# A hybrid decoder layer in split float32: feed-forward and per-layer gate by Strassen's scheme of seven products

## The chip, the core and the metric

The kernel runs on one core of one Trainium2 chip. The metric is the device time of one execution in microseconds (us), as a median of several runs. The core has TensorE for matmuls (PE in the profile; PEld is the loading of its stationary operand), VectorE (DVE), ScalarE (ACT), GpSimd (POOL) and SyncE (SP), whose queue issues nearly all transfers here. Matmul results stand in PSUM, in 8 banks of 128 x 512 float32.

## The reference

One decoder layer over 512 tokens of width 2048, all in float32:

```python
h = rms_norm(x, g_mix); z = h @ w_in
...                                     # attention and retention, 8 heads each
x = x + concatenate([a_out, r_out], axis=-1) @ w_o
h2 = rms_norm(x, g_ffn)
x = x + (silu(h2 @ w_gate) * (h2 @ w_up)) @ w_down        # 2048 -> 5632 -> 2048
gate = sigmoid(rms_norm(x, g_ple) @ w_ple_gate + b_ple_gate)   # 2048 -> 2048
x = x + (p @ w_ple_proj) * gate                           # 256 -> 2048
```

## The kernel before

Matmuls of full precision are made of three of the fast float32r kind. `split` (L50) writes a tile as H + L: ScalarE copies it to float32r (H, L54), VectorE subtracts (L, L55). `mm3` (L74) adds aH·bH, aH·bL and aL·bH in PSUM (L75 to L77), each 128 x 128 stationary against up to 512 moving columns. Weights arrive as units of 512 KB (128 x 1024 float32): `weights` (L60) loads one into `raw` from the SP queue and splits it into `wh` and `wl`, which have three buffers.

The residual stream lies in `xt` as 16 tiles [128 dims, 512 tokens], and `gained` (L127) makes the split activations `actH`, `actL` of a norm's input from it. `cols` (L101) computes [columns, tokens]: weights stationary, activations moving, four banks `acc` of 128 columns, which the last unit finishes one after the other. The norm's factor per token (`bc`) is multiplied in when a bank is read.

The feed-forward (L442 on) goes over 11 slices of 512 hidden columns. A slice is a `cols` for the gate (8 units), one for the up projection (8 units), and, one slice later, the down projection: four `cols` of 2 units each, whose banks are added into `xt` (L123). That is 192 matmuls each, 576 in a slice. Then come four column slabs of the per-layer gate (L490 on): `w_pp` with the embeddings `pTH` (24 matmuls), `w_pg` with the normed x (192), and the sigmoid with its products and the store. `tc` is a Tile context: it puts in the semaphores and orders each engine's instructions by its own estimate of the times. Every engine, and the SP queue, works through its list in order.

Of the kernel before, what the change touches and what calls it, by code (L numbers as in the profile page):

```python
# [33 lines left out]
def layer_kernel(ctx, tc, xT, pT, g_mix, wqk, wv, wg, qk_norm, g_ret, w_o, g_ffn,  # L34
                 w_gate, w_up, w_down, g_ple, w_pg, b_pg, w_pp,
                 ident_c, rope_c, ropeT_c, decay_c, mask_c, outT):
# [5 lines left out]
    actp = ctx.enter_context(tc.tile_pool(name="actp", bufs=NC))  # L42
    xp = ctx.enter_context(tc.tile_pool(name="xp", bufs=1))
    wp = ctx.enter_context(tc.tile_pool(name="wp", bufs=3))
    raw_pools = [ctx.enter_context(tc.tile_pool(name="rawp", bufs=2))]
    acc_p = ctx.enter_context(tc.tile_pool(name="acc_p", bufs=4, space=PSUM))
    tp_p = ctx.enter_context(tc.tile_pool(name="tp_p", bufs=2, space=PSUM))
    at_p = ctx.enter_context(tc.tile_pool(name="at_p", bufs=2, space=PSUM))

# [1 line left out]
    def split(H, L, src, scale=None):  # L51
        """H + L = src * scale, H the leading 12 bits of it and L the rest, exactly."""
# [21 lines left out]
    def mm3(o, aH, aL, bH, bL, start, stop):  # L74
        nc.tensor.matmul(o, aH, bH, start=start, stop=False)  # L75
        nc.tensor.matmul(o, aH, bL, start=False, stop=False)  # L76
        nc.tensor.matmul(o, aL, bH, start=False, stop=stop)  # L77
# [4 lines left out]
    def rows(units, act, evac, kc=2, then=None):  # L82
        """[tokens, columns]: the sum over the units' chunks, a bank for each token block."""
# [17 lines left out]
    def cols(units, act, evac, kc=2, late=1):  # L101
        """[columns, tokens]: a bank for each 128 columns, which the last units finish one by one."""
# [42 lines left out]
    def rms_of(src, parts, tmp, n, r):  # L145
        """Over the partitions of src: r[t, b] = (mean of token b * 128 + t + eps) ** -0.5."""
# [10 lines left out]
    def over_partitions(r):  # L157
        """[P, NB] -> every token's value on every partition."""
# [17 lines left out]
    bias = consts.tile([P, NC], F32)  # L176
# [6 lines left out]
    mix_ctx = ExitStack()  # L183
    mixp = mix_ctx.enter_context(tc.tile_pool(name="mixp", bufs=3))
    ap = mix_ctx.enter_context(tc.tile_pool(name="ap", bufs=1))

    # keeps the tensor engine busy from the start on, so that its clock gate opens
# [24 lines left out]
    bc1 = stat.tile([P, T], F32, name="bc", tag="bc", bufs=1)  # L212
# [3 lines left out]
    def load_rest():  # L216
# [4 lines left out]
        nc.sync.dma_start(bias, b_pg)  # L221
# [50 lines left out]
    def qk_attn(i, then=None):  # L272
        """q and k of a pair of heads as [tokens, d]: projection, norm, rotation."""
# [69 lines left out]
    def qk_ret(i):  # L343
        """q and k of a pair of heads as [d, tokens]: projection, norm, rotation."""
# [86 lines left out]
    h2T = []  # L431
    total = rp_tile("total")

    def after2(k):
        h2T.append(gained(k, gf))
# [3 lines left out]
    bc = stat.tile([P, T], F32, name="bc", tag="bc", bufs=1)  # L439
    norm_of(total, two_rm(), stat.tile([P, NB], F32, name="rs"), bc)  # L440
    mix_ctx.close()

# [1 line left out]
    h3T = []  # L444
    ep = ctx.enter_context(tc.tile_pool(name="ep", bufs=1))
    rawp2 = ctx.enter_context(tc.tile_pool(name="rawp2", bufs=2))
    total = ep.tile([P, T], F32)
    pTH = [[ep.tile([P, T], F32R, name=f"p{k}{part}") for part in "HL"] for k in range(2)]
    with tc.tile_pool(name="fp", bufs=1) as fp:
        for k in range(2):  # L450
            raw = fp.tile([P, T], F32, name="praw", tag="t", bufs=3)
            nc.sync.dma_start(raw, pT[k * P:(k + 1) * P, :])
            split(*pTH[k], raw)

        def after3(k):
            h3T.append(gained(k, gp))
            squares(total, k, ep.tile([P, T], F32, name="sq", bufs=2))

        def down(s, aT):
            add_into_x(lambda n: [w_down[2 * s + u, n] for u in range(2)], aT,  # L460
                       after3 if s == FS - 1 else None)

        prev = None
        for s in range(FS):
            sil, aT = [], []
            if s == 1:
                raw_pools.append(rawp2)
# [119 lines left out]
```

## Time and profile before

| | |
|---|---|
| median of 3 runs | 2536.45 us (2535.67 to 2536.95) |
| span of the profiled execution | 2533.9 us |
| TensorE busy | 2523.8 us, 12028 matmuls |
| VectorE busy | 1175.5 us |
| ScalarE busy | 733.8 us |
| HBM read / written | 241.47 MB / 4.19 MB |

The span runs from the first to the last instruction of the profiled execution; its time as a run counts some 2.5 us more around it. A matmul's duration in the trace overlaps with the next one's, so that the distance between starts, not the duration, tells how long TensorE needs for it.

### The profile page before, as it was taken

The page shows a single profiled execution, that of the slowest core. Times are in us where ns is not written, and L with a number is a line of the kernel's source. Part 1 is how long each engine was busy: PE and PEld are TensorE (multiplying, and loading weights), DVE is VectorE, ACT ScalarE, POOL GpSimd, SP SyncE. Part 2 cuts the span into 40 slices and gives each one's busy share as a digit, 9 for nine tenths or more (in the row PEclk, how much of TensorE's full clock was granted, in tenths as well). Part 3 has the DMA queues.
Part 4 walks back from the last instruction along what each step waited for, and adds up shares of the span by engine and source line. Part 5 has one row for each costly group of instructions (what it writes and reads, how often), then busy time and mean ns, then how long its engine had stood idle before and what let it go on. Part 6 is the DMA issues. An engine that isn't in the chain of part 4 may idle for free.

```text
span 2533.9 us, 29210 instructions
## 1 busy us (share of the span) xinstructions
PE 2523.8 (100%) x12028; PEld 2123.6 (84%) x12028; DVE 1175.5 (46%) x1611; ACT 733.8 (29%) x1058; POOL 134.6 (5%) x107
## 2 busy tenths in 40 slices
PE   9999999999999999999999999999999999999999
PEld 7888888888888888888888888888888888888887
DVE  6575674636364763333334242424242424347334
ACT  5333332323232442212222222222222222225322
POOL 1122020000000010000000000000000000000000
PEclk9999999999999999999999999999999999999999
DMA  5222222333323232232332332332322223323332
GB/s 188 84 84 82 85 92 97 103 100 102 108 94 109 88 124 96 97 100 92 100 100 92 100 99 92 100 97 94 100 95 97 96 97 98 100 93 99 111 113 75
DMA packets 74404, 251.75 MB, mean 99 GB/s; under 512 B 9120, under 2 KB 9760, under 8 KB 74272
## 3 DMA queue, kind: packets, MB, share of 16 engines
q1 hardware_dynamic: 71568, 245.69, 29.6%
q10 hardware_dynamic: 2704, 4.20, 0.7%
q8 instruction: 94, 1.54, 0.2%
q14 instruction: 38, 0.31, 0.0%
HBM read 241.47 MB, written 4.19 MB: 97 GB/s over the span
## 4 chain that ended last, share of the span: by engine, by line
PE 98%; DVE 1%; DMA 1%; issue 0%; SPq 0%; ACT 0%; DVEq 0%
PE acc L76 31%; PE acc L75 31%; PE acc L77 31%; PE at L76 1%; PE at L77 1%; PE at L75 1%; DMA x<-in_xT 0%; PE tp L334 0%; PE tp L309 0%; DVE x L123 0%; DVE wl L55 0%; PE tp L150 0%; PE tp L161 0%; DVE actL L58 0%; DMA gf<-in_g_ffn 0%
## 5 line engine op out<-in xcount | busy, mean ns | idle before, releaser
L55 DVE TENSOR_TENSOR wl<-raw,wh 128x1024 fp32r<-128x1024 f32 (+1 forms) x445 | 551.7, 1240 | 1064.0 <-ACT wh L54 1062.9
L54 ACT ACTIVATE wh<-raw 128x1024 fp32r<-128x1024 f32 (+1 forms) x445 | 470.6, 1058 | 1418.9 <-PE acc L76 1157.9
L75 PE MATMUL acc<-actH,wh 128*128 128x512 f32 x2048 | 797.3, 389 | 0.0
L76 PE MATMUL acc<-actL,wh 128*128 128x512 f32 x2048 | 797.2, 389 | 0.0
L77 PE MATMUL acc<-actH,wl 128*128 128x512 f32 x2048 | 793.9, 389 | 0.0
L77 PEld LDWEIGHTS acc<-actH,wl 128*128 128x128 f32 x2048 | 384.4, 188 | 79.6
L76 PEld LDWEIGHTS acc<-actL,wh 128*128 128x128 f32 x2048 | 384.5, 188 | 79.3
L75 PEld LDWEIGHTS acc<-actH,wh 128*128 128x128 f32 x2048 | 384.4, 188 | 79.2
L75 PE MATMUL acc<-aH,wh 128*128 128x512 f32 x704 | 273.9, 389 | 0.0
L76 PE MATMUL acc<-aL,wh 128*128 128x512 f32 x704 | 273.9, 389 | 0.0
L77 PE MATMUL acc<-aH,wl 128*128 128x512 f32 x704 | 272.2, 389 | 0.0
L76 PE MATMUL acc<-wl,actH 128*128 128x256 f32 (+1 forms) x768 | 244.7, 320 | 1.1 <-DVE wl L55 1.1
L77 PE MATMUL acc<-wh,actL 128*128 128x256 f32 (+1 forms) x768 | 244.2, 320 | 0.0
L123 DVE TENSOR_TENSOR x<-acc,x 128x512 f32<-128x512 f32 x304 | 207.7, 688 | 77.9 <-PE acc L77 76.1
L75 PE MATMUL acc<-wh,actH 128*128 128x256 f32 (+1 forms) x768 | 240.5, 321 | 1.6 <-ACT wh L54 1.6
L76 PEld LDWEIGHTS acc<-wl,actH 128*128 128x128 f32 x768 | 146.6, 191 | 11.9 <-DVE wl L55 1.6
L75 PEld LDWEIGHTS acc<-wh,actH 128*128 128x128 f32 x768 | 145.3, 191 | 12.5 <-ACT wh L54 2.5
L76 PEld LDWEIGHTS acc<-aL,wh 128*128 128x128 f32 x704 | 132.2, 188 | 27.5
L75 PEld LDWEIGHTS acc<-aH,wh 128*128 128x128 f32 x704 | 132.1, 188 | 27.4
L77 PEld LDWEIGHTS acc<-aH,wl 128*128 128x128 f32 x704 | 132.1, 188 | 27.4
L77 PEld LDWEIGHTS acc<-wh,actL 128*128 128x128 f32 x768 | 146.1, 191 | 10.2
L474 POOL TENSOR_TENSOR sil<-sil,bc 128x512 f32<-128x512 f32 x44 | 66.3, 1540 | 1213.2 <-ACT sil L473 1213.2
(136 smaller groups left out, 1615.6 us busy)
## 6 DMA issues: line engine op xcount, KB each, us to landing
raw<-in_w_gate SPq DMA_DIRECT2D x88, 512.0 KB, 3.6
raw<-in_w_up SPq DMA_DIRECT2D x88, 512.0 KB, 3.6
raw<-in_w_down SPq DMA_DIRECT2D x88, 512.0 KB, 3.6
raw<-in_wqk SPq DMA_DIRECT2D x63, 512.0 KB, 3.6
raw<-in_wv SPq DMA_DIRECT2D x32, 512.0 KB, 3.7
raw<-in_w_o SPq DMA_DIRECT2D x32, 512.0 KB, 3.6
raw<-in_w_pg SPq DMA_DIRECT2D x32, 512.0 KB, 3.7
raw<-in_wg SPq DMA_DIRECT2D x16, 512.0 KB, 3.7
```

Source lines behind the costliest of these rows:

```text
L54: nc.scalar.activation(H, src, AF.Copy)
L55: nc.vector.tensor_tensor(L, src, H.bitcast(F32), op=ALU.subtract)
L75: nc.tensor.matmul(o, aH, bH, start=start, stop=False)
L76: nc.tensor.matmul(o, aH, bL, start=False, stop=False)
L77: nc.tensor.matmul(o, aL, bH, start=False, stop=stop)
L123: nc.vector.tensor_tensor(xt[k], acc, xt[k], op=ALU.add)
L474: nc.gpsimd.tensor_tensor(g, g, bc, op=ALU.mult)
```

## The change

Attention and retention stay. The three matmuls of the feed-forward and the per-layer gate's are each cut into quarters, weights and activations both, and computed in Winograd's form of Strassen's scheme: seven products of quarter size in place of eight. With A (activations, [tokens, k]) and B (weights), quarters 11 to 22:

- The factors on the activations' side (`factors`): A11, S1 = A12 - A22 and so on, four differences on VectorE; each of the seven is split into H and L. For the feed-forward's input and the gate's they stay in SBUF (`s1` to `s7`), the factors of the hidden activations go to HBM (`spill`) and are fetched later by `reload`, 2 MB a product.
- The factors on the weights' side are made in place in the raw tiles, by four additions of 128 x 1024 (`Group.add`); `Group.extract` splits one of seven weight factors.
- Activations are stationary now and weights move, 512 columns: a result is [128 tokens, 512 columns]. A step (`Group.multiply`) is one product with one unit of 256 k: 12 matmuls. Three pairs of banks (X, Y, Z) take the seven products; sums that the scheme needs are partly made by going on in a bank, partly by `evacuate` on VectorE.
- Results have tokens in partitions, so that activations for the next matmul are transposed on TensorE (`to_factors`, L673), and x goes through HBM between stages (`xd`). The norm's factor is a scalar per partition (`rstd2`, `rstd3`).
- The order is a list of steps: at step i, `add` for step i+3, `extract` for i+2, `multiply` for i, and what `later` has put off.

A gate/up group (j, 11 of them) covers the 512 gate and 512 up columns of a slice with K = 2048 (4 units). The down projection is three blocks of k (4, 4, 3 units) times two column halves; the gate has two groups of 4 units.

```diff
+    def factors(a0, a1, sink):
+        lo, hi = slice(0, 256), slice(256, 512)
+        s1, s2, s3, s4 = (ev_tile("t", 4, 256, name) for name in ("t1", "t2", "t3", "t4"))
+        made = {"1": a0[:, lo], "5": s1, "6": s2, "3": s4, "7": s3, "2": a1[:, lo], "4": a1[:, hi]}
+        first = {"5": lambda: sub(s1, a0[:, hi], a1[:, hi]), "6": lambda: sub(s2, a0[:, lo], s1),
+                 "3": lambda: sub(s4, a1[:, lo], s2), "7": lambda: sub(s3, a1[:, hi], s2)}
+        for p in ORDER:
+            if p in first:
+                first[p]()
+            H, L, end = sink(p)
+            split(H, L, made[p])
+            end()
...
+        def add(self, p, u):
+            r = lambda q: self.raw[q, u]
+            if p == "5":
+                plus(r("11"), r("11"), r("12"))
+            elif p == "6":
+                plus(r("11"), r("11"), r("22"))
+            elif p == "7":
+                plus(r("12"), r("12"), r("22"))
+                self.load("21", u)
+            elif p == "4":
+                plus(r("11"), r("11"), r("21"))
+                self.load_next("22", u)
+        def extract(self, p, u):
+            wh = wq.tile([P, 2, T], F32R, name="wh", tag="wh")
+            wl = wq.tile([P, 2, T], F32R, name="wl", tag="wl")
+            split(wh, wl, self.raw[SOURCE[p], u])
...
+            for b in range(2):
+                at = slice(b * P, (b + 1) * P)
+                for c in range(2):
+                    s = self.tiles[p][:, 2 * u + c]
+                    mm3(self.bank[k][b], s[:, 0, at], s[:, 1, at], wh[:, c, :], wl[:, c, :],
+                        first and c == 0, last and c == 1, p in "237")
...
+                    elif p == "6":
+                        sub(g.v[b], Y[b], g.e1[b])
+                    elif p == "3":
+                        plus(g.v[b], Z[b], g.v[b])
+                        finish(*quarter, b, g.v[b], early[b])
+                    elif p == "7":
+                        sub(g.e1[b], Y[b], g.e1[b])
+                        plus(g.e5[b], g.e5[b], g.e1[b])
+                        finish(*quarter, b, g.e5[b], early[b])
...
+    for i in range(NC // 2):
+        pair = []
+        for k in (2 * i, 2 * i + 1):
+            t = ev_tile("A")
+            nc.scalar.activation(t, xt[k], AF.Copy, scale=gf[:, k:k + 1])
+            pair.append(t)
+        factors(*pair, into(s_h2, i))
...
+    def reload(tiles, where, n, wait={}):
+        def go(p):
+            tiles[p] = sp.tile([P, 8, 2, 256], F32R, name="s" + p, tag="s" + p)
+            nc.sync.dma_start(tiles[p][:, :n].bitcast(F32), where[p].bitcast(F32))
+        return lambda p: later(wait[p], lambda: go(p)) if p in wait else go(p)
...
-            cols([w_gate[s, u] for u in range(NC // 2)], h2T, gate_evac)
-            cols([w_up[s, u] for u in range(NC // 2)], h2T, up_evac)
-            if prev is not None:
-                down(*prev)
-            prev = (s, aT)
-        down(*prev)
...
+        for n, act in ((3, "add"), (2, "extract"), (0, "multiply")):
+            if 0 <= i + n < len(steps):
+                g, p, u = steps[i + n]
+                getattr(g, act)(p, u)
+        for fn in due.pop(i, []):
+            fn()
+        i += 1
```

**How instructions stand on VectorE in the feed-forward.** Before, in a late slice, splits of weight units (`wl`) and the four banks `acc` of the gate, multiplied by `bc` into `t`, follow each other:

```order
L55 TENSOR_TENSOR wl_15242<-raw_15240,wh_15241 128x1024
L55 TENSOR_TENSOR wl_15272<-raw_15270,wh_15271 128x1024
L471 TENSOR_TENSOR t_15216<-acc_14972,bc_7965 128x512
L471 TENSOR_TENSOR t_15221<-acc_14973,bc_7965 128x512
L471 TENSOR_TENSOR t_15226<-acc_14974,bc_7965 128x512
L471 TENSOR_TENSOR t_15231<-acc_14975,bc_7965 128x512
L55 TENSOR_TENSOR wl_15302<-raw_15300,wh_15301 128x1024
L55 TENSOR_TENSOR wl_15332<-raw_15330,wh_15331 128x1024
```

Now, some steps after the end of a gate/up group, additions of weights (L468, `raw`), splits of weight factors (L59, `wl`), and the differences (`t1` to `t4`) and split remainders (`o`) of the finished activations stand mixed:

```order
L59 TENSOR_TENSOR wl_11516<-raw_11322,wh_11515 128x1024
L59 TENSOR_TENSOR o_11489<-tp_11473,o_11489 128x256
L465 TENSOR_TENSOR t1_11485<-tp_11473,A_11483 128x256
L468 TENSOR_TENSOR raw_11301<-raw_11301,raw_11272 128x1024
L468 TENSOR_TENSOR raw_11207<-raw_11207,raw_11337 128x1024
L59 TENSOR_TENSOR wl_11540<-raw_11343,wh_11539 128x1024
L468 TENSOR_TENSOR raw_11322<-raw_11322,raw_11295 128x1024
L465 TENSOR_TENSOR t2_11486<-tp_11473,t1_11485 128x256
L59 TENSOR_TENSOR wl_11600<-raw_11363,wh_11599 128x1024
L59 TENSOR_TENSOR o_11493<-t1_11485,o_11493 128x256
L468 TENSOR_TENSOR raw_11343<-raw_11343,raw_11316 128x1024
```

Between two splits, each for one step of TensorE, there now stand additions of the same size and the factors of the group before.

**How TensorE's list goes on after the last output projection.** Before, its last matmul (`mixH`) is followed by the gate's (the names are those of the bank, the split activations and the weights):

```order
L77 MATMUL acc_7902<-mixH_7697,wl_7905 128x512
L75 MATMUL acc_8008<-actH_7737,wh_8013 128x512
L76 MATMUL acc_8008<-actL_7738,wh_8013 128x512
L77 MATMUL acc_8008<-actH_7737,wl_8014 128x512
L75 MATMUL acc_8008<-actH_7744,wh_8013 128x512
L76 MATMUL acc_8008<-actL_7745,wh_8013 128x512
```

Now transposes of x (L659) stand there, and then the steps of the first group:

```order
L659 MATMUL tp_8238<-ident_88,x_4_102 128x128
L659 MATMUL tp_8238<-ident_88,x_5_103 128x128
L659 MATMUL tp_8238<-ident_88,x_6_104 128x128
L659 MATMUL tp_8238<-ident_88,x_7_105 128x128
L79 MATMUL X0_8373<-wh_8359,s1_7935 128x512
L79 MATMUL X1_8374<-wh_8359,s1_7935 128x512
L80 MATMUL X0_8373<-wl_8360,s1_7935 128x512
L81 MATMUL X0_8373<-wh_8359,s1_7935 128x512
L79 MATMUL X0_8373<-wh_8359,s1_7935 128x512
```

What moved is that the factors `s1` to `s7` of x stand between the last addition into x and the products. On VectorE all eight pairs of chunks (88 operations of 256 columns) come before the weights' split for the third product.

**The fetched factors on the SP queue**, in the last gate/up group (`s1` to `s7` are the fetched tiles, `a2` the spilled ones, `raw` weights):

```order
L710 DMA s6_14885<-a0_6_7944 128x4096
L497 DMA a2_1_7956<-o_14725 128x512
L519 DMA raw_14948<-in_w_gu 128x1024
L497 DMA a2_5_7957<-o_14729 128x512
L519 DMA raw_14971<-in_w_gu 128x1024
L497 DMA a2_6_7958<-o_14733 128x512
L519 DMA raw_14933<-in_w_dn 128x1024
```

Before, this queue held units of weights alone in the feed-forward; now weights stand behind spills, which wait for VectorE, and behind fetches, which wait for TensorE.

## Rows read from the trace of the kernel before

**Rows 1.** The page: span, and busy time of each engine.
```profile
span 2533.9 us, 29210 instructions
PE 2523.8 (100%) x12028; PEld 2123.6 (84%) x12028; DVE 1175.5 (46%) x1611; ACT 733.8 (29%) x1058; POOL 134.6 (5%) x107
```

**Rows 2.** The page: chain that ended last, by engine.
```profile
PE 98%; DVE 1%; DMA 1%; issue 0%; SPq 0%; ACT 0%; DVEq 0%
```

**Rows 3.** Waits of TensorE: in total, times, longest.
```profile
PE acc L75 <- ACT wh L54: 1.6, 1, 1.6
...
PE acc L75 <- DVE x L123: 0.5, 1, 0.5
```

**Rows 4.** A window of the feed-forward: us, busy time and count, clock, DMA share, GB/s.
```profile
900.00:2300.00 1400.00, 1400.00 (x6180) 1159.25 (x6179) 531.22 (x578) 333.39 (x364) 67.34 (x45) 1.00 0.30 98
```

**Rows 5.** Timeline of TensorE where the feed-forward begins: start, duration.
```profile
894.09 0.39 PE L77 MATMUL acc<-mixH,wl 128*128 128x512 f32 x1
894.32 0.39 PE L75 MATMUL acc<-actH,wh 128*128 128x512 f32 x1
```

**Rows 6.** Timeline of TensorE: eight transposes between matmuls.
```profile
257.64 1.03 PE L309 MATMUL tp<-ident,z 128*128 128x128 f32 x8
258.43 0.48 PE L75 MATMUL acc<-mixH,wh 128*128 128x512 f32 x1
```

**Rows 7.** Groups of instructions by shape: busy us, mean ns, idle time before.
```profile
L55 DVE TENSOR_TENSOR wl<-raw,wh 128x1024 fp32r<-128x1024 f32 x443 | 550.4, 1242 | 1064.0 <-ACT wh L54 1062.9
L54 ACT ACTIVATE wh<-raw 128x1024 fp32r<-128x1024 f32 x443 | 469.3, 1059 | 1418.8 <-PE acc L76 1157.9 <-issue 156.2 <-PE acc L77 84.3
L123 DVE TENSOR_TENSOR x<-acc,x 128x512 f32<-128x512 f32 x304 | 207.7, 688 | 77.9 <-PE acc L77 76.1
L55 DVE TENSOR_TENSOR PL<-pt,PH 128x256 fp32r<-128x256 f32 x16 | 6.7, 419 | 1.9 <-ACT PH L54 1.9
```

**Rows 8.** Timeline of VectorE while instructions queue: start, duration.
```profile
887.71 0.69 DVE L123 TENSOR_TENSOR x<-acc,x 128x512 f32<-128x512 f32 x1
888.31 1.22 DVE L55 TENSOR_TENSOR wl<-raw,wh 128x1024 fp32r<-128x1024 f32 x1
889.44 0.69 DVE L140 TENSOR_TENSOR total<-total,sq 128x512 f32<-128x512 f32 x1
890.04 0.75 DVE L58 SCALAR_TENSOR_TENSOR actL<-x,gf,actH 128x512 fp32r<-128x512 f32 x1
890.71 0.69 DVE L123 TENSOR_TENSOR x<-acc,x 128x512 f32<-128x512 f32 x1
```

**Rows 9.** Timeline of ScalarE while instructions queue.
```profile
877.36 0.62 ACT L137 ACTIVATE total<-x 128x512 f32<-128x512 f32 x1
877.88 1.04 ACT L54 ACTIVATE wh<-raw 128x1024 fp32r<-128x1024 f32 x1
878.83 0.71 ACT L57 ACTIVATE actH<-x,gf 128x512 fp32r<-128x512 f32 x1
```

**Rows 10.** TensorE after its early waits: a window (clock: 0.50), and its timeline.
```profile
21.00:23.80 2.80, 2.64 (x6) 2.15 (x7) 2.80 (x7) 2.80 (x6) 0.00 (x0) 0.50 0.96 243
...
22.61 0.63 PE L76 MATMUL acc<-wl,actH 128*128 128x512 f32 x1
23.03 0.63 PE L77 MATMUL acc<-wh,actL 128*128 128x512 f32 x1
```

**Rows 11.** Transfers: the first 20 us as a window; KB and us to landing.
```profile
0.00:20.00 20.00, 17.22 (x62) 11.55 (x62) 13.80 (x23) 16.49 (x27) 0.20 (x4) 1.00 0.90 320
raw<-in_w_gate SPq DMA_DIRECT2D x88, 512.0 KB, 3.6
x<-in_xT SPq DMA_DIRECT2D x16, 256.0 KB, 6.3
```

**Rows 12.** End of the chain, in order of time: start, us.
```profile
2528.51 0.43 DVE gt L509
2530.66 0.33 DVEq L583
```

More of the change, by code (lines that the diff above doesn't have):

```diff
@@ L445, in layer_kernel @@
[L445 to L449, printed above, removed]
+    pool = lambda name, bufs, side="left", **kw: tc.tile_pool(name=name, bufs=bufs, side=side,
+                                                              reuse_waits="tile", **kw)
+    sp = ctx.enter_context(pool("sp", 1))
@@ new lines, in into, with spill, sink, later @@
+    def into(tiles, k):
+        return lambda p: (tiles[p][:, k, 0, :], tiles[p][:, k, 1, :], lambda: None)
+    def spill(where, k):
+        def sink(p):
+            o = late_pools["ev2"].tile([P, 2, 256], F32R, name="o", tag="o", bufs=4)
+            return o[:, 0, :], o[:, 1, :], lambda: later(1, lambda: nc.sync.dma_start(where[p][:, k].bitcast(F32), o.bitcast(F32)))
+        return sink
+    now = [0]
+    due = {}
+    steps = []
+    def later(n, fn):
+        due.setdefault(now[0] + n, []).append(fn)
@@ new lines, in layer_kernel, with __init__, load, add @@
+    class Plain:
+        def __init__(self, n):
+            self.n, self.then = n, None
+            steps.append((self, "p", 0))
+        def load(self):
+            self.raw = raw_ab.tile([P, 2, T], F32, name="raw", tag="l1")
+            nc.sync.dma_start(self.raw, w_pp[self.n])
+        def add(self, p, u):
+            pass
+        def extract(self, p, u):
+            self.wh = wq.tile([P, 2, T], F32R, name="wh", tag="wh")
+            self.wl = wq.tile([P, 2, T], F32R, name="wl", tag="wl")
+            split(self.wh, self.wl, self.raw)
+            self.then()
+        def multiply(self, p, u):
+            for b in range(NB):
+                o = tp_p.tile([P, T], F32, name="tp", tag="tp")
+                at = slice(b * P, (b + 1) * P)
+                for c in range(2):
+                    mm3(o, pTH[c][0][:, at], pTH[c][1][:, at], self.wh[:, c, :], self.wl[:, c, :],
+                        c == 0, c == 1)
+                t = ev_tile("g", 4, name="pp")
+                nc.scalar.activation(t, o, AF.Copy)
+                nc.sync.dma_start(ppd[b][:, self.n], t)
@@ new lines, in to_factors @@
+    def to_factors(get, k0, sink, gain=None):
+        tps = []
+        for k in (k0, k0 + 1):
+            tp = tp_p.tile([P, T], F32, name="tp", tag="tp")
+            for b in range(NB):
+                nc.tensor.transpose(tp[:, b * P:(b + 1) * P], get(b)[:, k * P:(k + 1) * P], ident)
+            tps.append(tp)
+        a1 = ev_tile("A")
+        if gain is None:
+            nc.scalar.activation(a1, tps[1], AF.Copy)
+            factors(tps[0], a1, sink)
+        else:
+            a0 = ev_tile("A")
+            nc.scalar.activation(a0, tps[0], AF.Copy, scale=gain(k0))
+            nc.scalar.activation(a1, tps[1], AF.Copy, scale=gain(k0 + 1))
+            factors(a0, a1, sink)
@@ L450, in layer_kernel, with load_p @@
+    first = [0, 4, 8, 11]
+    for kg in range(3):
+        for n in range(2):
+            after = lambda p: None
+            if n == 1:
+                after = reload(s_d[kg + 1], s_a[kg + 1], KG[kg + 1]) if kg < 2 else reload(s_e, s_h3, 4, {"1": 4, "5": 1})
+            groups.append(Group(lambda kh, nh, u, n=n: w_dn[n, kh, nh, u], range(first[kg], first[kg + 1]),
+                                s_d[kg], down(kg, n), None, after))
+    pTH = []
+    bias_t = []
+    def load_p():
         for k in range(2):
-            raw = fp.tile([P, T], F32, name="praw", tag="t", bufs=3)
+            raw = ev_tile("A")
@@ L452, in layer_kernel @@
             nc.sync.dma_start(raw, pT[k * P:(k + 1) * P, :])
+            pTH.append([late_pools["ev2"].tile([P, T], F32R, name="pT", tag="o", bufs=4) for _ in range(2)])
             split(*pTH[k], raw)
[L455 to L461, printed above, removed]
@@ new lines, in layer_kernel @@
+    for n in range(2):
+        groups.append(Group(lambda kh, nh, u, n=n: w_pl[n, kh, nh, u], range(4), s_e, gate(n),
+                            split_order if n == 0 else None))
+    for a, b in zip(groups, groups[1:]):
+        a.next = b
+    groups[-3].plains = plains
+    for n, pl in enumerate(plains):
+        pl.then = lambda n=n: groups[-2].load("11", n)
+    for q in ("11", "12", "22"):
+        for u in range(4):
+            groups[0].load(q, u)
+    p_at = steps.index((groups[-3], "7", 0))
@@ L523, in _constants @@
+    b_at = steps.index((groups[-2], "3", 0))
+    i = -3
+    while i < len(steps) or due:
+        now[0] = i
+        if i == p_at:
+            load_p()
+        if i == b_at:
+            load_bias()
+        for n, act in ((3, "add"), (2, "extract"), (0, "multiply")):
[5 more added lines that the diff above has]
+        i += 1
 def _constants():
```

279 lines of the change are left out of this document (205 added, 74 removed).

## The prediction

> **What bounds the kernel now.** I read the page first. TensorE is busy for the whole span, VectorE for 46% of it and ScalarE for 29% [rows 1]; the chain that ended last is TensorE for 98%, nearly all of it the three matmul lines of `mm3` [rows 2]. The table of waits then shows that this is no accident of averages: TensorE waited for another engine four times, between 0.5 and 1.6 us each [rows 3]. So what counts is how many matmuls there are and how far apart they start. From 900 to 2300 us, 6180 matmuls of 512 columns take 1400 us, which is 0.2265 us from start to start [rows 4]. The part that the change rewrites begins at 894.3 us, where the last output projection hands over to the first gate matmul without a gap [rows 5], and its last matmul starts at about 2528 us. It has 7200 matmuls (11 slices of 192 + 192 + 192, then 768 + 96), and 7200 x 0.2265 = 1631 us fills that stretch. Everything before 894 us stays in the same order on every engine, so I take it as unchanged.
>
> **TensorE's own work.** A gate/up group of the new code has 7 products of 4 units with 12 matmuls, 336 in place of 384. Eleven of them make 3696; the down projection has 1848 (11 x 2 x 7 x 12), the per-layer gate 672, its projection 96 as before. That is 6312, or 888 fewer: 888 x 0.2265 = **-201.1 us**. The old norms lose 8 transposes and 2 matmuls, -1.3 us. New are 304 transposes of 128 x 128: 64 for the copy of x, 176 for the activations, 64 for the last x. Eight of them take 0.87 us (258.43 minus 257.64, and a little of the first one's start) [rows 6], so 0.109 each and **+33.1 us**. TensorE's work falls by 169.3 us in all.
>
> **VectorE in a gate/up group.** This is the work that pays for the products. A group now has 28 exact splits of a 128x1024 tile (7 products, not 4 quarters, and `extract` splits each), 16 additions of whole weight tiles, 10 operations of 512 columns on the banks, 4 of `scalar_tensor_tensor`, and 22 of 256 columns for the factors of two activation blocks. I have two prices for each. The durations are 1.242, 0.688 and 0.419 us for 1024, 512 and 256 columns [rows 7], and 0.75 us for `scalar_tensor_tensor` [rows 8]. Between instructions that queue up, the next one starts earlier: 0.60 us after a 512-column one and 1.13 us after a 1024-column one, 0.66 after `scalar_tensor_tensor` [rows 8]; for 256 columns the same slope gives 0.335 us as an estimate. The additions aren't in the trace of before; their nearest row is the split of the same size, and they can hardly be cheaper than its 1.13 or dearer than its 1.25. By starts a group costs 44 x 1.13 + 10 x 0.60 + 4 x 0.66 + 22 x 0.335 = 65.7 us, by durations 73.7 us. TensorE's time for the group is 336 x 0.2265 + 16 x 0.109 = 77.8 us. I take the starts, because VectorE will be queued all the time. So TensorE keeps the lead, but with 12 us to spare where it had 80 us of VectorE's idle time in 131 us before.
>
> The average hides a burst. A split for step i+2 can begin when step i-1 has freed one of the three `wh` buffers, and must be there 2 steps (5.4 us) later; the ScalarE half takes 1.06 and the VectorE half 1.24 us [rows 7], so VectorE may run some 3 us late. Adding up the order of VectorE after a group's end step by step (2.26 us in a step with an addition, against 2.72 us of TensorE), I find the backlog at 2.5 to 4 us where the factors of the last group fall among the additions. I put 1.5 us of stall on each of the 11 groups, **+17 us**; 0 if the transposes cover it, 70 if the next part is right. ScalarE is no bound: 28 x 0.95 and some 26 small ones make about 36 us of 78 [rows 9].
>
> The Trainium skill ("VectorE: DVE Perf Modes", section "The DRAIN you can't avoid") says that after every operation the pipeline must empty before the next one starts, so queued instructions gain nothing. By that the durations are the price, and a group costs VectorE 73.7 us plus its waits. The trace speaks against it [rows 8], so it is a rival below and not the sum.
>
> **The start of the new part.** Before, the first gate matmul needs only what the last addition into x leaves chunk by chunk. Now the factors of all 16 chunks come first: VectorE's order puts six additions of squares, the norm, and then 84 operations of 256 columns, 5 splits and 6 additions before the split that product "6" waits for. From 895 us (last addition into x) that is 6 x 0.60 and about 3.5 us for the norm, to 902; then 84 x 0.335 + 11 x 1.13 = 40.6 us, to 943 if VectorE never waits. But the chunks' copies have two buffers and the differences four, so one pair's factors can hardly begin before the last pair's are read: each pair alternates between ScalarE (two scaled copies, seven splits, two copies of x's transposes, about 4.4 us) and VectorE (3.7 us), and I add 1 us a pair for that, 950 us. TensorE has 64 transposes and four steps to do in the 56 us, 18 us of work. **+38 us** (30 if nothing waits, 55 if the two engines hardly overlap). After the hole the clock may have to come back: at 21 to 23.8 us, after waits, it stood at 0.50 (1.2 of 2.4 GHz) and six matmuls started 0.43 us apart [rows 10], 1.2 us more than at 0.2265. I put this at **+2 us**.
>
> **Transfers.** Factors and x go through HBM now: 22 pairs x 7 tiles of 256 KB out and back, x four times out and back, in all some 140 MB more. In a common group this is 12 MB in 78 us, 156 GB/s, where the core has moved 320 GB/s at a share of 0.90 [rows 11]. But as each product of the last gate/up group and of every second down group ends, 2 MB of new factors are fetched: 27 MB in a group, 345 GB/s, about what the engines can do. Weights queue behind on SP. A weight tile lands in 3.6 us, a smaller one took 6.3 us in the crowd at the start [rows 11]; the tightest weights ("11", four steps, 10.9 us) have room for one such delay. **+10 us** over four groups (0 to 40). In the last two down groups VectorE has 62.6 us (33 x 1.13 + 18 x 0.60 + 44 x 0.335) against 60.4 of TensorE, and the two gate groups 71 against 76: **+8 us** (0 to 25). The end is a sum of five operations on a 512-column bank where it was four on half a bank [rows 12]: **+2 us**.
>
> **The sum.** 2533.9 - 169.3 + 38 + 2 + 17 + 10 + 8 + 2 = 2441.6 us of span. The median of the runs stands 2.5 us over the profiled span, so **2444 us**.
>
> **Rivals.**
> *VectorE is the bound of the gate/up groups.* For it: its order has chains (difference, ScalarE's split, remainder), each a wait. Against it: rows 8. With 73.7 us and some 8 us of waits a group takes 82 us, 4.4 more than TensorE's 77.8: 48 us over 11 groups instead of 17, and by the same prices 4 more in each of the four last groups: about 2490 us.
> *Nearly everything is hidden.* The order was laid out by a scheduler that interleaves the factors with the splits; if the backlog stays under 3 us everywhere and the weights land in time, what is left is the hole at the start, perhaps 30 us: 2533.9 - 169.3 + 30 + 2 + 5 + 2.5 = 2404 to 2415 us.
> *Weights late everywhere, slower than before.* SP issues in order, and spills that wait for VectorE stand ahead of weights. The forecast leaves 92 us to the old time; 152 loads of the tight kinds (8 a group, 19 groups) would have to hold TensorE up for 0.6 us each. That begins where a 512 KB load takes over 10.9 us instead of 3.6. At 156 GB/s I see no reason for it: about 2550 us.
> *The fetches of factors cost more*, 40 us instead of 10: 2474 us.
>
> **Chances.** The forecast with its neighbourhood, 2420 to 2465, 0.52; the expensive fetches 0.10; VectorE as the bound 0.17; nearly all hidden 0.16; late weights 0.05. The range from 2405 to 2496 leaves out the last case and the edges of two others. A measurement of this kernel can tell some 0.2% (5 us) from no change; faster 0.94, same 0.01, slower 0.05.
>
> **What the profile would show.** Right: 6312 matmuls of `mm3` behind 894 us, 0.2265 us apart; a hole of about 55 us with little TensorE work, in which VectorE and ScalarE alternate on 256-column tiles; then VectorE 85 to 95% busy with TensorE's waits at 1 to 2 us a group, mostly for `wl`. Wrong: a gate/up group that lasts over 80 us, TensorE waiting for `wl` in most steps (VectorE as the bound); waits of `wh` or of an addition for a transfer of `raw` (late weights or fetches); a hole outside 30 to 55 us; a matmul pitch that isn't 0.2265 us because the stationary side is now a slice of a wider tile.

## The result and the profile after

The changed kernel takes 2470.02 us (median of 4 runs, 2469.8 to 2471.33) against 2536.06 us before on the same chip: a ratio of 0.9741, with a 95% interval of 0.9727 to 0.9754. That is 66 us less where the forecast had 92 less, and lies inside the forecast's range, 26 us above its value. It lies above the neighbourhood that the forecast gave itself, 2420 to 2465 us, and next to one of its rivals, the dear fetches of factors (2474 us, chance 0.10).

The page of the changed kernel first: the span, the busy time of each engine, and the chain that ended last. They answer to [rows 1, 2].

```profile
span 2468.3 us, 30337 instructions
...
PE 2385.4 (97%) x11434; PEld 1994.3 (81%) x11434; DVE 1836.6 (74%) x2469; ACT 1091.5 (44%) x1628; POOL 70.3 (3%) x63
...
PE 85%; DVE 6%; DMA 5%; ACT 2%; issue 1%; ACTq 0%; SPq 0%; DVEq 0%
```

TensorE still leads, but VectorE went from 46% to 74%, and 15% of the chain lies outside TensorE where it was 2%. The table of TensorE's waits, which had four of at most 1.6 us in [rows 3], now has long ones (engine, line, for whom: us in total, times, longest):

```profile
PE Y L79 <- ACT wh L58: 18.9, 4, 16.3
PE tp L79 <- ACT pT L58: 16.9, 2, 10.0
PE tp L79 <- ACT pp L601: 6.5, 2, 6.3
PE tp L154 <- ACT sqs L58: 6.0, 1, 6.0
PE X L80 <- DVE wl L59: 5.7, 6, 2.4
```

`Y` is the bank of product "6", so the 16.3 us belong to the start of the new part. `tp` with `pT` and `pp` is the projection between the last down group and the gate. The windows say the same by stage: two gate/up groups, the first down group, the last one, the projection, the first gate group (us, then busy time and count of PE, PEld, DVE, ACT, POOL, then clock, DMA share, GB/s).

```profile
1020.00:1098.00 78.00, 78.00 (x353) 64.49 (x352) 67.20 (x80) 39.95 (x52) 0.00 (x0) 1.00 0.48 155
1098.00:1176.00 78.00, 78.00 (x354) 64.48 (x353) 67.20 (x81) 39.99 (x52) 0.00 (x0) 1.00 0.49 155
1802.70:1886.10 83.40, 80.73 (x349) 65.33 (x350) 71.78 (x86) 38.65 (x50) 0.00 (x0) 0.98 0.66 228
2180.70:2240.00 59.30, 58.90 (x266) 48.07 (x265) 57.45 (x83) 35.72 (x59) 0.00 (x0) 1.00 0.70 246
2240.00:2283.40 43.40, 19.44 (x61) 13.57 (x59) 8.13 (x11) 14.99 (x29) 0.00 (x0) 0.72 0.86 338
2283.40:2379.70 96.30, 92.80 (x408) 75.41 (x409) 83.69 (x118) 57.40 (x88) 1.01 (x1) 0.98 0.48 166
```

In a common gate/up group TensorE never stops, at a VectorE busy for 67.2 of 78 us. In the 43 us of the fifth row TensorE has 19 us of work, at a clock of 0.72, with VectorE busy for 8 us and the DMA engines at 338 GB/s.

To see what each term of the forecast became, I went through TensorE's timeline from the last output projection (892.0 us) on. From one start to the next I took off 0.2266 us for a matmul and 0.109 for a transpose; the rest is lost time, waits and the slow clock behind them alike. All 6312 matmuls are there, and a gate/up group without a wait comes to 78.1 us (forecast 77.8).

```
stretch                                       forecast   lost, us
start of the new part, first group            38 + 2     44.0
the other ten gate/up groups                  17         4.1
the first four down groups (factor fetches)   10         12.2
last two down groups with the projection  \   8          33.2
two gate groups                           /              11.2
behind the last matmul, more than before      2          2.3
```

The forecast's 10 us were for four groups with fetches: the last gate/up group, the second and the fourth down group, and the last down group. The first three fall into the second and third rows, the fourth into the row below. The forecast came to 77, the measurement to 107. The part ahead of 892 us ended 2.1 us earlier than in [rows 5]. One term is off by 36 us, the last groups. Another, the pacing of the gate/up groups, is off by 13 the other way.

### The profile page after: what moved, and what is told of

Read it like the earlier page. It is cut to its first block, busy times and chain, and to the rows that moved or that the text cites. A ratio compares the mean times of both kernels' runs of the same rounds, so it can differ in the third digit from the quotient of the medians.

```text
span 2468.3 us, 30337 instructions
## 1 busy us (share of the span) xinstructions
PE 2385.4 (97%) x11434; PEld 1994.3 (81%) x11434; DVE 1836.6 (74%) x2469; ACT 1091.5 (44%) x1628; POOL 70.3 (3%) x63
## 4 chain that ended last, share of the span: by engine, by line
PE 85%; DVE 6%; DMA 5%; ACT 2%; issue 1%; ACTq 0%; SPq 0%; DVEq 0%
PE acc L80 10%; PE acc L81 10%; PE acc L79 10%; PE Y L80 7%; PE Y L79 7%; PE Y L81 7%; PE Z L80 5%; PE Z L81 5%; PE Z L79 5%; PE X L81 5%; PE X L80 5%; PE X L79 5%; DVE wl L59 2%; DVE raw L468 2%; PE at L80 1%
## 5 line engine op out<-in xcount | busy, mean ns | idle before, releaser
L58 ACT ACTIVATE wh<-raw 128x1024 fp32r<-128x1024 f32 (+1 forms) x667 | 705.9, 1059 | 946.3 <-PE Y L81 225.2
L59 DVE TENSOR_TENSOR wl<-raw,wh 128x1024 fp32r<-128x1024 f32 (+1 forms) x667 | 811.8, 1222 | 367.5 <-ACT wh L58 365.3
L468 DVE TENSOR_TENSOR raw<-raw 128x1024 f32<-128x1024 f32 x296 | 358.1, 1222 | 28.6 <-DMA raw<-in_w_gu 14.7
L80 PE MATMUL Y<-wl,s 128*128 128x512 f32 x888 | 349.6, 394 | 0.3 <-DVE wl L59 0.3
L81 PE MATMUL Y<-wh,s 128*128 128x512 f32 x888 | 346.9, 391 | 0.0
L79 PE MATMUL Y<-wh,s 128*128 128x512 f32 x888 | 311.6, 392 | 18.9 <-ACT wh L58 18.9
L80 PE MATMUL Z<-wl,s 128*128 128x512 f32 x592 | 234.3, 396 | 3.5 <-DVE wl L59 3.4
L81 PE MATMUL X<-wh,s 128*128 128x512 f32 x592 | 232.1, 393 | 1.8 <-DVE s L59 1.8
L81 PE MATMUL Z<-wh,s 128*128 128x512 f32 x592 | 230.8, 391 | 0.0
L79 PE MATMUL X<-wh,s 128*128 128x512 f32 x592 | 210.1, 394 | 5.3 <-ACT wh L58 5.0
L79 PEld LDWEIGHTS Y<-wh,s 128*128 128x128 f32 x888 | 167.2, 189 | 55.2 <-ACT wh L58 20.4
L79 PE MATMUL Z<-wh,s 128*128 128x512 f32 x592 | 208.7, 393 | 0.9 <-ACT wh L58 0.9
L81 PEld LDWEIGHTS Y<-wh,s 128*128 128x128 f32 x888 | 167.4, 189 | 34.0
L79 PE MATMUL acc<-actH,wh 128*128 128x512 f32 x384 | 149.9, 390 | 0.0
```

The costliest lines, as they stand in the source:

```text
L58: nc.scalar.activation(H, src, AF.Copy)
L59: nc.vector.tensor_tensor(L, src, H.bitcast(F32), op=ALU.subtract)
L79: nc.tensor.matmul(o, aH, bH, start=start, stop=False, skip_group_check=goes_on)
L80: nc.tensor.matmul(o, aH, bL, start=False, stop=False, skip_group_check=goes_on)
L81: nc.tensor.matmul(o, aL, bH, start=False, stop=stop, skip_group_check=goes_on)
L468: nc.vector.tensor_tensor(o, x, y, op=ALU.add)
```

## Experiments: the hole before the gate

**Order of the queue, or the transfers.** Four views of the changed kernel show how the hole comes about. SP's timeline while the hole opens (start, duration):

```profile
2227.67 0.33 SPq L771 DMA_DIRECT2D A<-in_pT  x1
2230.71 0.33 SPq L710 DMA_DIRECT2D s<-h  x1
...
2248.74 0.39 SPq L771 DMA_DIRECT2D A<-in_pT  x1
...
2254.08 0.97 SPq L710 DMA_DIRECT2D s<-h  x2
...
2263.89 0.81 SPq L602 DMA_DIRECT2D pp<-pp  x2
```

ScalarE's, with what ended its idle time:

```profile
2246.20 1.06 ACT L58 ACTIVATE wh<-raw 128x1024 fp32r<-128x1024 f32 x1 [3.28 <-DMA raw<-in_w_pp]
2247.17 0.61 ACT L58 ACTIVATE pT<-A 128x512 fp32r<-128x512 f32 x1
...
2260.05 0.63 ACT L58 ACTIVATE pT<-A 128x512 fp32r<-128x512 f32 x1 [6.41 <-DMA A<-in_pT]
...
2273.07 1.22 ACT L601 ACTIVATE pp<-tp 128x512 f32<-128x512 f32 x2 [4.55 <-DMA pp<-pp]
```

TensorE's:

```profile
2247.83 0.80 PE L79 MATMUL tp<-wh,pT 128*128 128x512 f32 x1 [6.90 <-ACT pT L58]
...
2260.73 0.80 PE L79 MATMUL tp<-wh,pT 128*128 128x512 f32 x1 [9.97 <-ACT pT L58]
...
2273.72 0.79 PE L79 MATMUL tp<-wh,pT 128*128 128x512 f32 x1 [6.29 <-ACT pp L601]
```

And the transfers of that crowd, 2206 to 2272 us (KB each, median us to landing), with the mean rate:

```profile
DMA packets 7938, 23.98 MB, mean 363 GB/s; under 512 B 888, under 2 KB 888, under 8 KB 7039
...
s<-h SPq DMA_DIRECT2D x7, 1024.0 KB, 10.1
...
A<-in_pT SPq DMA_DIRECT2D x2, 256.0 KB, 8.6
...
pp<-pp SPq DMA_DIRECT2D x2, 256.0 KB, 9.2
```

The DMA engines are full while the hole lasts, and TensorE comes back into step when they no longer are (two windows, with the clock, the DMA share and GB/s at the end):

```profile
2256.00:2266.00 10.00, 5.01 (x13) 3.54 (x14) 0.69 (x1) 1.71 (x3) 0.00 (x0) 0.55 1.03 421
2272.00:2283.00 11.00, 8.98 (x32) 6.96 (x32) 0.00 (x0) 4.13 (x7) 0.00 (x0) 0.70 0.42 163
```

The first wait is put down to `pT`, but the first half of `pT` was issued at 2227.7 us and landed at 2233.7 us. In ScalarE's list its split stands behind that of a weight tile of the projection, for whose transfer ScalarE waited 3.28 us. The second half of `pT` is issued 21 us behind the first and lands 11 us later. The third wait is for a buffer of `pp`, whose store takes 9.2 us. So transfers come late; but does one come late because of its place in the queue, or because the DMA engines are full? The first theory, Q, was the queue. I brought `pT` forward:

```
-            pTH.append([late_pools["ev2"].tile([P, T], F32R, name="pT", tag="o", bufs=4) for _ in range(2)])
+            pTH.append([s_d[2]["24"[k]][:, i] for i in (6, 7)])
...
-    p_at = steps.index((groups[-3], "7", 0))
+    p_at = steps.index((groups[-4], "7", 0))
```

> The changed kernel, but the activations of the projection (pT) are fetched and split some 30 steps earlier, during the first of the two last down groups, into slots that the six-unit factor tiles leave empty; nothing else moves. Theory Q (the two fetches come late because they stand in SP's in-order queue behind spills and factor fetches, and their split halves need the spills' buffers): TensorE's waits of 7.1 and 10.4 us for pT go, and the 6.5 us for pp behind them shrinks, so 18 to 25 us less than 2470: 2445 to 2452. Rival B (the transfers as such are the bound there, 340 to 430 GB/s with 7 MB of factors due): what comes earlier only makes the factors or gate weights later, the hole moves behind the projection: 2463 to 2475.

Measured: 2472.74 us (2471.25 to 2474.57), no gain. TensorE's waits from 2230 to 2400 us in this run:

```profile
PE tp L79 <- ACT pp L601: 20.8, 4, 16.2
PE X L79 <- ACT s L58: 4.2, 1, 4.2
```

The waits for `pT` are gone, and the next thing the projection needs from the DMA engines, the stores that free the buffers of `pp`, takes their place with 16.2 us. The last down group with the projection loses 28.5 us where it lost 32.2, and the first gate group 7 us more than before. Theory Q's time is out, and rival B, the transfers, had it right; but the stores of `pp` stand in SP's queue too, so that the queue isn't excluded yet. Next, the whole projection away from the crowd:

```
+            if (kg, n) == (1, 1):
+                plains = [Plain(n) for n in range(NS)]
...
-    groups[-3].plains = plains
+    groups[13].plains = plains
...
-        pl.then = lambda n=n: groups[-2].load("11", n)
+        pl.then = lambda n=n: groups[14].load("11", n)
```

> The changed kernel, but the projection's four steps (96 matmuls, its weights and pT) stand between the two down groups of the second chunk, where no factors are fetched and no spills run, instead of between the last down group and the gate. Theory Q expects the projection to cost its 21.8 us of matmuls and no more there, and the hole of 30 us between the last down group and the gate to go with it: 2440 to 2448. Rival C (the projection is the cover under which the last x becomes factors: some 12 us of sums and squares, transposes and 22 operations of 256 columns after the last product): the gate waits for its units 2 and 3 after 16 us of work on units 0 and 1, a new hole of 8 to 15 us: 2452 to 2462. Rival B (transfers are the bound): the 7 MB of factors now have 22 us less to land in, the hole stays at 20 us or more: 2460 to 2475.

Measured: 2446.09 us (2444.2 to 2449.94), 24 us less than the changed kernel. In its trace the projection loses nothing at the new place (the two groups around it lose 5.1 us, 5.2 before), and the last down group loses 1.5 us in place of 32.2. The first gate group loses 15.6 us, 9 more than it did: rival C, the cover, is right about most of these 9. The time lies in theory Q's range and outside those of C and B. It doesn't prove the queue, since the move takes the projection away from the full DMA engines as well. The gate's first group (a window as above) and the waits from 2255 to 2365 us:

```profile
2263.50:2360.10 96.60, 84.26 (x371) 68.06 (x370) 86.15 (x123) 54.18 (x84) 14.29 (x1) 0.96 0.69 250
```

```profile
PE X L79 <- ACT s L58: 5.8, 1, 5.8
...
PE Z L79 <- DMA s<-h: 1.7, 1, 1.7
```

The fetched factors cost 1.7 us, although the DMA engines moved 352 GB/s from 2229 to 2295 us here too. So the crowd itself costs little; the projection stood in it with data that were needed first and issued among data needed later. To tell the issuing queue from the DMA engines I left the projection in its place and had ScalarE issue its transfers:

```
-                nc.sync.dma_start(ppd[b][:, self.n], t)
+                nc.scalar.dma_start(ppd[b][:, self.n], t)
...
-            nc.sync.dma_start(raw, pT[k * P:(k + 1) * P, :])
+            nc.scalar.dma_start(raw, pT[k * P:(k + 1) * P, :])
```

> The changed kernel, but the projection's two fetches of pT and its sixteen stores of pp are issued by ScalarE instead of standing in SP's in-order queue; everything else stays where it was. After the last runs two readings are left of the 30 us hole before the gate. Theory O (the order: what the projection needs stands in SP's queue behind 1 MB fetches and spills, and each issue there also waits for the transfer eight places before it): both fetches go out when their buffers are free, the stores at once, the waits for pT fall from 17 to under 6 us and the one for pp (6.5) goes: 2446 to 2455. Rival B (the DMA engines: at 340 to 430 GB/s a transfer takes some 10 us whoever issues it, and ScalarE now waits too): 2463 to 2475.

Measured: 2465.29 us (2464.78 to 2467.11). The waits of 2230 to 2290 us:

```profile
PE tp L79 <- ACT pT L58: 12.9, 2, 9.5
PE tp L79 <- ACT pp L601: 5.1, 2, 4.8
```

A fetch of `pT` still takes 6.7 us to land and the first two stores of `pp` 8 to 11. By the trace 2.5 us of the gain lie in the hole and 3 in the start of the new part, which the edit doesn't touch.

```profile
A<-in_pT ACTq DMA_DIRECT2D x2, 256.0 KB, 6.7
```

The run changes the queue, but hardly the order. The second fetch of `pT` went out at 2247.8 us (2248.7 in the changed kernel), within 0.1 us of the landing of the transfer issued eight places before it. The program's transfers take turns on eight semaphores, whichever queue issues them. Of the 55 issued in the crowd of the changed kernel none went out before the eighth before it had landed, and 21 followed that landing within 0.15 us. So another queue alone is worth 2.5 us of the hole, and the order of issue and the DMA engines are not told apart by it. Last, the same number of transfers with fewer bytes (the scheduler's order came out a little different, with 16 transfers between the two fetches of `pT` in place of 21):

```
+            if where is s_h3:
+                nc.sync.dma_start(tiles[p][:, :n, 0].bitcast(F32), where[p][:, :, 0].bitcast(F32))
+                nc.gpsimd.memset(tiles[p][:, :n, 1].bitcast(F32), 0.0)
+                return
```

> The changed kernel, but of the factors of the last x that go through HBM (the first half, four pairs) only the high halves are written out and fetched back; the low halves are set to zero by GpSimd, so the per-layer gate leaves out the low part of half of its activations. That takes 3.7 MB of stores and 3.7 MB of fetches from the crowd between 2206 and 2272 us and leaves the order, the queues and the number of transfers as they are. Theory B (16 DMA engines full at about 390 GB/s; what the projection needs lands when the bytes ahead of it have gone): the 5.5 to 7.3 MB that lie in the crowd are 14 to 18 us, so the hole falls from 30 to 12 to 18 us and the time to 2452 to 2459. Rival O (order and buffers alone: each wait is a chain of issue, landing, split and store): the chains stay, under 6 us gained, 2464 to 2470.

Measured: 2456.74 us (2455.59 to 2464.47), 13 us less; the last down group with the projection loses 21.6 us where it lost 32.2. The crowd of 2206 to 2272 us, where a fetch of factors (now 512 KB) lands in 7.5 us:

```profile
DMA packets 11111, 19.69 MB, mean 298 GB/s; under 512 B 945, under 2 KB 6193, under 8 KB 11107
...
s<-h SPq DMA_DIRECT2D x7, 512.0 KB, 7.5
```

The crowd is over earlier: the DMA engines are no longer full from 2258 us on, where it was 2272 before.

```profile
2246.00:2256.00 10.00, 4.99 (x11) 3.51 (x12) 2.57 (x4) 3.13 (x7) 0.00 (x0) 0.50 1.05 391
2258.00:2268.00 10.00, 5.51 (x23) 4.13 (x23) 1.23 (x1) 3.66 (x6) 0.00 (x0) 1.00 0.62 215
```

4.3 MB fewer in the crowd are some 12 us at 363 GB/s, and 10.6 us of the hole went (3 more of the gain lie in the start, untouched here too). That is more than rival O allowed and less than theory B had forecast. So about a third of the hole goes with these bytes, as far as the changed order lets one say. How the other 21.6 us divide between the bytes that are left, the order of issue and the buffers of `pp` isn't shown.

## Experiments: how much VectorE has to spare

The forecast put 1.5 us of stalls on each gate/up group; 0.2 to 0.5 came (1.7 in the last). One more VectorE operation of 224 columns per step, on a tile nobody reads, then two:

```
             self.w[p, u] = wh, wl
+            for _ in range(1 if self in groups[:FS] else 0):
+                plus(pad, pad, pad)
```

> The changed kernel, and in each of the 28 steps of every gate/up group one more VectorE operation of 224 columns on a tile of its own that nothing reads. By the 0.335 us from start to start at 256 columns and 0.60 at 512 it costs 0.30 us, 8.5 us a group. Theory N (VectorE was busy 67.2 of 78.1 us in a group, so there are 11 us to spare and bursts are absorbed by the three weight buffers): 75.7 us still fit, groups stay at 78.1 to 78.6 us: 2470 to 2477. Rival P (the forecast's 17 us: the backlog comes in bursts, and less slack makes each burst a stall): 1 to 3 us a group, 2481 to 2505.

> As the run with one operation, with two in each step: 17 us more VectorE work a group, 84.2 us against TensorE's 78.1. Theory N: VectorE now sets the pace, a group takes 84 to 85 us, 6 to 7 more in each of the eleven: 2535 to 2550. Rival P (bursts come on top of the full load): 87 us or more a group, above 2565. If the groups stay near 78 us, VectorE's busy time isn't what counts there: about 2475.

Measured: 2486.88 us (2484.78 to 2489.73) and 2504.61 us (2503.38 to 2509.01). Neither run tests what it should. The operations were free to run ahead of their steps: in both some 35 ran in a full group (88 in the first), until they were used up, and each such group took 80.2 us with VectorE busy for 77.5 of 80. I tied each operation to its step by letting it read the step's `wl`:

```
-                plus(pad, pad, pad)
+                plus(pad, pad, wl[:, 0, :224].bitcast(F32))
```

> The runs with padding let the extra operations run ahead of their steps, 35 to a group. Here each reads the step's own weight remainder, so that there is exactly one per step, 28 a group, 8.5 us by starts. Theory N (VectorE has 10.9 us to spare in a group and the weight buffers absorb the bursts): 75.7 us of 78.1, no more than 0.6 us a group lost: 2470 to 2478. Rival P (bursts): with 35 a group 2.1 us were lost, so 1 us or more with 28: 2481 to 2495.

> The same with two tied operations in each step, 56 a group: 67.2 plus 17 is 84.2 us of VectorE against TensorE's 78.1. Theory N (VectorE's starts set the pace as soon as they exceed TensorE's time): groups of 84 to 86 us, 6 to 8 us more in each of eleven, 2535 to 2560. Rival: if operations were charged by their durations of 0.385 us, the group would come to some 89 us and the time to 2590; if groups stay at 80 us, VectorE is not what paces them.

Measured: 2494.92 us (2493.8 to 2498.05) and 2564.11 us (2561.3 to 2567.18). With 28 a group takes 80.7 to 80.8 us, with 56 mostly 87 to 88.6. A window of each, one operation first:

```profile
1130.00:1210.00 80.00, 78.77 (x352) 64.08 (x350) 74.80 (x107) 39.21 (x53) 0.00 (x0) 1.00 0.45 151
```

```profile
1130.00:1210.00 80.00, 77.39 (x339) 61.93 (x339) 77.71 (x124) 37.78 (x47) 0.00 (x0) 1.00 0.45 145
```

With 8.5 us more work, 2.7 us a group are lost although VectorE is idle for 5 of 80: rival P is right there and theory N wrong. That the loss comes in bursts is what P says; the runs show only that it comes before VectorE is full. With 17 us more, VectorE sets the pace: busy for 77.71 of 80 us, it works 84.6 in a group of 87.1, which is the 84.2 by starts, and some 3 us come on top; the time is above theory N's range and below the rival's price by durations. So a loss as the forecast's exists, but begins between VectorE's 67.2 us and 75.7; at 67.2 it costs nothing, I take it because the three weight buffers absorb it.

## Experiments: the hole at the start

TensorE's timeline of the changed kernel, and the windows before and behind 931 us:

```profile
929.88 1.31 PE L659 MATMUL tp<-ident,x 128*128 128x128 f32 x8
947.53 1.22 PE L79 MATMUL Y<-wh,s 128*128 128x512 f32 x2 [16.34 <-ACT wh L58]
```

```profile
907.00:931.00 24.00, 20.91 (x90) 15.79 (x88) 20.43 (x44) 19.86 (x46) 0.00 (x0) 0.80 0.65 251
931.00:952.00 21.00, 2.00 (x5) 1.00 (x4) 19.74 (x46) 16.30 (x37) 0.00 (x0) 0.56 0.42 142
```

Product "6" begins at 947.5 us, where the forecast said 950. VectorE is busy for 40 of 45 us, ScalarE for 36. Half of the factors put under the first steps:

```
+    for i in range(4):
+        pair_of(i)
+    for n in range(2):
+        x_rows(n)
+    for i in range(4):
+        due[i] = [lambda i=i: pair_of(4 + i)]
+    for n in range(2):
+        due[4 + n] = [lambda n=n: x_rows(2 + n)]
```

> The changed kernel, but only the first four pairs of chunks of x become factors before the first group; the other four pairs, and the second half of x's transposed copy, are emitted between the first steps, which work on the first four pairs alone. To allow it x lies in buffers that the later weights and evictions take over one by one. Theory V (the hole of 44 us at the start is VectorE's 84 operations of 256 columns, 42 of them now under the first six steps): 42 x 0.335 = 14 us and half of the waits between the engines go, 12 to 18 us less: 2452 to 2458. Rival S (the hole is a latency of ScalarE and VectorE alternating, or the weights 22 that wait for x's memory, or all of VectorE's work comes due again a few steps later): under 5 us, 2465 to 2471.

Measured: 2463.18 us (2461.57 to 2465.9), 7 us less. The hole is 33.3 us, 10.7 less; neither forecast of the experiment held, since VectorE is still busy for 19 of the 21 us from 931 to 952: its work comes due again a few steps later, and TensorE's matmuls wait in small pieces. Next, a part of VectorE's work on GpSimd:

```
+            if p in pool:
+                nc.scalar.activation(H, made[p], AF.Copy)
+                nc.gpsimd.tensor_tensor(L, made[p], H.bitcast(F32), op=ALU.subtract)
```

> The changed kernel, but in the start's factors the remainders of the four products 3, 7, 2 and 4 (32 of VectorE's 84 operations of 256 columns) are made by GpSimd. Theory V (VectorE's count bounds the hole): 32 x 0.335 = 10.7 us less if GpSimd takes under 1.3 us each beside it: 2459 to 2463. Rival G (GpSimd is so slow, or slows VectorE so much while both work, that its chain of 32 sets the end): nothing gained or some 10 us lost, 2468 to 2482. No run so far shows a GpSimd operation of this kind, so I hold both possible.

Measured: 2475.23 us (2474.94 to 2475.83), 5 us more. In the profiled run 4.2 of these lie ahead of the change, where the last output projection ends at 896.3 us in place of 892.0; behind it the run loses 104.7 us and the changed kernel 104.2. So nothing was gained, and hardly anything lost. Groups of VectorE from 902 to 951 us of this run, then one of the changed kernel from 902 to 947, then of GpSimd from 890 to 960 (count, busy us, mean ns; idle before):

```profile
L465 DVE TENSOR_TENSOR t<-A,t 128x256 f32<-128x256 f32 x21 | 13.5, 667 | 0.6
L59 DVE TENSOR_TENSOR s<-t,s 128x256 fp32r<-128x256 f32 x16 | 8.8, 581 | 0.0
```

```profile
L465 DVE TENSOR_TENSOR t<-A,t 128x256 f32<-128x256 f32 x21 | 8.3, 421 | 0.1
```

```profile
L490 POOL TENSOR_TENSOR s<-A,s 128x256 fp32r<-128x256 f32 x16 | 13.5, 866 | 8.6 <-ACT s L489 8.5
```

GpSimd would be fast enough, but the operations that stay on VectorE take 0.54 to 0.67 us in place of 0.42. The third run takes x's transposed copy out:

> The changed kernel without the transposed copy of x at the start of the new part: the 64 transposes and ScalarE's 16 copies are left out and x goes out as it lies, so the residual that comes back later is not x in the right layout; the stores stay. Theory V (VectorE's 84 operations set the hole; TensorE has time in it and ScalarE is beside): 0 to 5 us less, 2465 to 2470. Rival S (ScalarE's 28 us in the hole, 8 of them these copies, are in the chain): 8 to 12 us less, 2458 to 2462.

Measured: 2462.09 us (2459.69 to 2464.03), 8 us less, against theory V. Product "6" starts 47.3 us behind the last output projection, where it was 55.5. Windows over this stretch, the changed kernel first:

```profile
892.03:947.53 55.50, 27.56 (x117) 20.42 (x115) 45.48 (x103) 42.35 (x95) 1.01 (x1) 0.72 0.54 187
```

```profile
895.13:942.36 47.23, 17.78 (x53) 11.54 (x51) 44.74 (x103) 35.86 (x79) 1.11 (x1) 0.67 0.41 143
```

So the copies, 8 us of ScalarE with the transposes that they wait for, were in the chain: VectorE waited for scaled copies and splits that stood behind them. VectorE is idle for 10.0 us of the stretch in the changed kernel and for 2.5 us without the copies. The hole is the length of two engines in turn, and without the copies nearly VectorE's count alone.

**Both gains together**: the projection moved and the half start, in one kernel.

> The two edits that gained, together: the projection between the two down groups of the second chunk, and half of the start's factors under the first six steps. They touch stretches 1100 us apart, so the gains should add: 2446 minus 7, 2436 to 2442. The rival is that one run's gain was a shift of the front part of the program, which varied by some 4 us from kernel to kernel: 2443 to 2448.

Measured: 2440.08 us (2439.81 to 2443.07), a ratio of 0.9621 (0.9606 to 0.9635) to the kernel before. The gains of 24 and 7 us add. This version beats both kernels.

## Why the forecast was right, and where it was not

**The matmuls.** Right: 6312 of them, 0.2266 us apart, the stationary side as a slice of a wider tile notwithstanding.

**VectorE in a group.** 67.2 us against 65.7 worked out by starts. The starts hold; [rows 8] have their answer in the changed kernel:

```profile
1102.81 1.22 DVE L468 TENSOR_TENSOR raw<-raw 128x1024 f32<-128x1024 f32 x1
1103.95 1.22 DVE L59 TENSOR_TENSOR wl<-raw,wh 128x1024 fp32r<-128x1024 f32 x1
1105.08 1.22 DVE L468 TENSOR_TENSOR raw<-raw 128x1024 f32<-128x1024 f32 x1
```

An addition of whole tiles costs what the split costs, 1.13 us, as assumed. The rival by durations (2490 us) is out. The Trainium skill ("VectorE: DVE Perf Modes", section "The DRAIN you can't avoid") says that the next operation doesn't start until the pipeline is empty; these rows don't agree. It also says that a next operation that is not held starts earlier, which the prediction left out; with that the rows agree.

**Pacing of the gate/up groups, +17**: measured 4. A loss of this size exists, as the tied operations show, but it begins above the load that the change brings. The backlog of 2.5 to 4 us that I had added up seems to fit into the two steps (5.4 us) that a split may take; that reading is argued, the zero is measured.

**The start, +38 and +2**: measured 44 (41 to 42 in the other runs that left it alone). The time of product "6" came out within 3 us, by the right two engines.

**Fetches in the down groups, +10**: measured 12. **The end, +2**: 2.3.

**The last groups, +8**: this term was mis-sized; it measured 44. It had been worked out from VectorE and TensorE alone. The forecast did say that the fetches ask for as much as the DMA engines move, and the last down group was among the four groups that it priced at 10 us together, but only for weights that queue behind fetches. What else passes the DMA engines there was left out: the factors of the last x go out and come back while the projection's weights, `pT` and `pp` pass through them, and what is needed first stands among what is needed last. The runs price it: when the projection goes elsewhere, 31 us of the last down group come back and the gate loses 9, in the main what the projection had covered, and the time falls by 24; when 4.3 MB are taken out, 10.6 us of the hole go.

**The rival that came nearest.** The rival of dear fetches put 40 us on the fetches in place of 10 and came to 2474 us. Its size is close: 12 us in the first four down groups and 31 around the projection. It had a chance of 0.10, and it named no projection.

**Luck.** The time came out 26 us above the forecast because the pacing of the gate/up groups cost 13 us less than forecast while the last groups cost 36 more. Without the first error it would have been some 39 us above.

**Not settled**: the stalls of 1 to 3 us at the start of each down group, and how the hole before the gate divides between bytes and order.

## What to carry to other kernels

Price the DMA engines by stage, as the computing engines are: where a stage asks for all they move, list what it needs first and see what is issued ahead of it; here a load brought forward alone only handed its wait to the next transfer. A stretch of matmuls that needs little from outside is cover, and is worth most where neither queue nor engine is crowded. An engine with 86% of the pace-setting one's work cost next to nothing here, with 97% (75.7 of 78.1 us) it cost 2.7 us a group: slack is used up before the averages meet.

## What was unexpected in the hardware

- GpSimd beside VectorE: 256-column operations took 0.85 us on GpSimd, and those on VectorE with it 0.54 to 0.67 us on the mean, against 0.42 alone. The Trainium skill ("GPSIMD Engine Reference", section "1. Specifications") names contention between the two where VectorE's operation has two inputs in SBUF; this run agrees, all of these operations having two.
- The DMA engines moved 363 GB/s over 66 us of fetches, stores and weights in the changed kernel, where [rows 11] had 320 GB/s; a 1 MB fetch then took 10.1 us to land and a 256 KB one 8.6.
- The part ahead of the change, the same in all kernels, ended between 891.4 and 896.3 us in the profiled runs: 5 us that no edit explains, and as much as some of the gains above.
